# The rest of the second layer's modulation, moved from the first layer's down projections to the second layer's input projection

## The chip, the core and the metric

The kernel runs on one core of a Trainium2 chip. The metric is the device time of one launch in microseconds (us), and lower is better. The core has a matrix engine (PE, with its weight loads shown apart as PEld), VectorE (DVE), ScalarE (ACT), GpSimd (POOL), and SyncE (SP), whose queue issues nearly all DMA transfers of this program. All engines run side by side, each one through its own instructions in order, and they wait for one another by semaphores.

## The reference, cut to what matters

One step of a two-layer trunk over 1152 tokens (128 context tokens and 1024 latent ones) of width 1024. Each layer is

```python
sh1, sc1, gt1, sh2, sc2, gt2 = split(silu(c) @ w_ada + b_ada)      # modulation, for c and for c_ctx
y = rmsnorm(x, g1) * (1 + sc1) + sh1
x = x + gt1 * (mixers(y @ w_in) @ w_out)                            # attention, mLSTM, attention
y = rmsnorm(x, g2) * (1 + sc2) + sh2
a, g = split(y @ w_up)
x = x + gt2 * ((silu(conv(g)) * a) @ w_down)                        # gated FFN
```

The modulation of a layer depends on `c` and `c_ctx` and on its own weights alone, so it can be computed at any time before its first use. `sh1` and `sc1` are used when the layer begins, the other four after that layer's mixers.

## The kernel before, in words

Everything is kept transposed: 128 channels on the partitions, tokens along the free dimension, in three chunks of 384 tokens. Products are made to nearly full float32 precision by splitting each factor into a high part and a low part (`split`, L104: ACT casts the high part, L108; DVE or POOL subtracts it for the low part, L109) and by three matmuls per product. Weights come through `weight` (L111): one 512 KB transfer into a staging tile `stg` (2 buffers), ACT makes `wh`, POOL makes `wl` (4 buffers each).

The order of the work is that of the calls in the source. The framework's scheduler may interleave what is independent; an instruction wrapped in `pin` stays behind all that was traced before it on its engine. A DMA waits on SP's queue until the buffer that it fills is free, and everything behind it on that queue waits with it.

The stages that matter here, in order of time:

- **First layer's input projection** (`project_a` with l = 0). Nine slots of projection and mixer preparation; first-layer modulation is woven between them (`modulation`, L210): 64 steps, each a 256 KB transfer of transposed `w_ada` rows into `stm` and two DVE instructions of 128x512 (L221) that multiply by the broadcast silu(c) row `cb` and sum along the free dimension. `MODS` sets how many steps each slot takes.
- **First layer's up projections** (`Up.run`). 22 steps of matmuls; `Up.modulation` (L1426) gives the second layer's modulation as a list of 96 units of the same kind (48 groups of 128 outputs by two halves of the 1024 inputs; L1453, two pinned DVE instructions per unit), and `some_mod` takes 52 of them here.
- **First layer's down projections** (`down_units`, L1533). For each of the three token chunks, 22 steps of 24 matmuls (L1556) into all eight PSUM banks. Each step's `fetch` (L1538) loads a `w_down` tile and a 128x384 tile `hst` of the hidden activations and splits both; four buffers of each lie ahead of PE. After each step, `some_mod` takes what is left of the modulation, 44 units over 63 steps. In a step that takes a unit, the low part of `hst` (`hs`, L109) is made on POOL, in the others on DVE. At the end of a chunk DVE adds the eight PSUM banks to `x` (L1603); the next chunk's matmuls need the banks free. The norm for the second layer (L308 and L311 among others) is spread over the next chunk's steps.
- **Second layer's input projection** (`project_a` with l = 1), with no modulation in it.
- The second layer's mixers, out projection, up projections, and its **down projections**: the same code as in the first layer, with no modulation left to do and a lighter final norm (L1619).

The units' tiles (`stm`, three buffers; `cb`, one; `mjk`, one; the sums `mds`) lie in a pool `md`, which is released after the down projections. `half(h)` (L1440) loads one half of `cb` and applies Silu on ACT; the sums of the first input half go into the modulation tile itself, and `fin` adds both halves and the bias.

Of the kernel before, what the change touches and what calls it, by code (L numbers as in the profile page):

```python
# [50 lines left out]
def kernel(ctx: ExitStack, tc: tile.TileContext, A, O, layers=L):  # L51
# [458 lines left out]
        return [unit(i, c) for c in range(3) for i in range(2)], tiles  # L510


    def project_a(S, l, y, Z, first):
        vec = vecs[l]

        count, free = [0], []
# [199 lines left out]
        if l == 0:  # L716
            cb = conditioning(S)
            mod = [u for i in range(2, 6) for u in modulation(S, l, i, cb)]
        done = 0
        for i, slot in enumerate(slots):  # L720
            upto = sum(MODS[:i + 1]) * len(mod) // sum(MODS)
            weave(slot, mod[done:upto])
            done = upto

# [498 lines left out]
    class Up:  # L1223
# [196 lines left out]
                share -= unit  # L1420
                f()

        def mods_left(self):
            return sum(u for u, f in self.mod)

        def modulation(self, mp):  # L1426

            l = self.l + 1
            groups = [range(16), range(16, 48)]
            loads = [(h, m) for ms in groups for h in range(2) for m in ms]  # L1430
            wq, st = [], dict(s=(mods[l], mp.tile([128, 48, 2], F32, tag="mds", name="mds", bufs=1)))

            def load():
                if loads:
                    h, m = loads.pop(0)
                    w = mp.tile([128, 512], F32, tag="stm", name="stm", bufs=3)
                    sync.dma_start(out=w, in_=A["w_adat"][l, m, :, h * 512:(h + 1) * 512])
                    wq.append(w)

            def half(h):  # L1440
                def f():
                    st["cb"] = mp.tile([128, 2, 512], F32, tag="cb", name="cb", bufs=1)
                    sync.dma_start(out=st["cb"], in_=A["crow"][:, h * 512:(h + 1) * 512].unsqueeze(0).to_broadcast([128, 2, 512]))
                    act.activation(out=st["cb"], in_=st["cb"], func=AF.Silu)
                return 0, f

            def unit(h, m):
                def f():
                    load()
                    w = wq.pop(0)  # L1450
                    for j in range(2):
                        o = w if j else mp.tile([128, 512], F32, tag="mjk", name="mjk", bufs=1)
                        pin(dve.scalar_tensor_tensor(out=o, in0=w, scalar=1.0, in1=st["cb"][:, j], op0=ALU.mult, op1=ALU.mult,  # L1453
                                                     accum_out=st["s"][h][:, m, j:j + 1]))
                return 1, f

            def fin(ms):
                def f():
                    a, b = (t[:, ms.start:ms.stop] for t in st["s"])
                    bias = vecs[l][:, V_BADA + ms.start:V_BADA + ms.stop]  # L1460
                    dve.tensor_tensor(out=b, in0=a, in1=b, op=ALU.add)
                    dve.tensor_tensor(out=a, in0=b, in1=bias.unsqueeze(2).to_broadcast([128, len(ms), 2]), op=ALU.add)
                return 0, f
            load()
            load()
            return [u for ms in groups for u in [v for h in range(2) for v in [half(h)] + [unit(h, m) for m in ms]] + [fin(ms)]]

        def run(self):
            S, l = self.S, self.l
            oq, tn = self.ops[:2]  # L1470
            sq2, rstd2, scale2 = self.norm()
            S.rings = dict(sA=[0, 1], sB=[2, 3], sD=[4, 5], u1=[6, 7])
            self.bk = {}
            run(sq2)
            rstd2[0]()
            rstd2[1]()
            run(scale2)
            dbg(f"xm{l}", self.x)
            tn.release()
            oq.release()  # L1480
            fp = self.new_pool("f", "left")
            self.mp = None
            if l + 1 < layers:
                self.mp = self.new_pool("md", "left")
                self.mod = self.modulation(self.mp)
                self.some_mod(0)

            def tiles():
                self.tiles = {k: fp.tile([128, n], F32, tag=k, name=k, bufs=1) for k, n in (("gb", 1156), ("lb", T), ("tg", 1156))}
                conv_pad(self.tiles["gb"])  # L1490
            for n in range(NFF):
                tiles()
                nxt = n + 1 < NFF
                if n == 0:
                    for p in ("P1", "P6", "P2", "P5", "P7", "C22", "P3", "P4", "C21"):
                        self.step(n, p)
                    self.load(1)
                    self.step(n, "G2")
                    self.prep(1, "g")
                    self.step(n, "L2")  # L1500
                    self.prep(1, "s")
                    self.prep(1, "t1")
                else:
                    self.prep(n, "a")
                    self.step(n, "P1")
                    if nxt:
                        self.load(n + 1)
                    self.step(n, "G2")
                    self.step(n, "P2")
                    self.step(n, "P6")  # L1510
                    if nxt:
                        self.prep(n + 1, "g")
                    self.some_mod(2)
                    self.step(n, "P7")
                    self.step(n, "P5")
                    self.step(n, "C22")
                    if nxt:
                        self.prep(n + 1, "s")
                    self.some_mod(1 - n % 2)
                    self.step(n, "L2")  # L1520
                    self.step(n, "P3")
                    if nxt:
                        self.prep(n + 1, "t1")
                    self.step(n, "P4")
                    self.step(n, "C21")
                if n + 1 < NFF:
                    self.tail(n)
            self.p5.release()
            self.p4.release()
            self.p3.release()  # L1530
            return fp

    def down_units(S, l, x, Z, hp, up, scale):  # L1533
# [4 lines left out]
        def fetch(lo_eng=dve):  # L1538
            if len(ready) == len(steps):
                return  # L1540
            c, k = steps[len(ready)]
            wt = weight(A["w_down"][l, k])
            s = S.t.tile([128, CH], F32, tag="hst", name="hst", bufs=3)
            sync.dma_start(out=s, in_=Z.h[k, :, csl(c)])
            h = hp.tile([128, 2, CH], F32R, tag="hs", name="hs", bufs=4)
            split(s, h[:, 0], h[:, 1], act, lo_eng)
            ready.append((*wt, h))
# [31 lines left out]
            fetch()  # L1579
        up.tail(NFF - 1)  # L1580
        fetch()
        rs, left, nmod = {}, [], up.mods_left()
        for c in range(3):
            D = {}
            for k in range(NFF):
                for m in range(8):
                    mul(D, c * NFF + k, m)
                i, total = c * NFF + k, len(steps) - 3
                share = (i + 1) * nmod // total - i * nmod // total if i < total else 0
                if k < NFF - 1:  # L1590
                    fetch(pool if share else dve)
                up.some_mod(share)
                if left and k in (1, 2) or k > 3:
                    run(left[:1])
                    del left[:1]
            if c == 2:
                S.rings = dict(u1=list(range(8)))
            acc = {}
            squares, rstd = stat_units(S, x, c, rs, acc)
            for m in range(8):  # L1600
                for a, b, j in pieces(c):
                    xs = x[:, m, c * CH + a:c * CH + b]
                    dve.scalar_tensor_tensor(out=xs, in0=D[m][:, a:b], scalar=mods[l][:, 40 + m, j:j + 1], in1=xs, op0=ALU.mult, op1=ALU.add)  # L1603
                squares[m]()
                if m == 3:
                    fetch(pool)
            left = (rstd if c == 2 else stats(c, acc)) + scale(c, rs)
        assert not up.mod
        return left

    def final_units(x, c, rs):
# [31 lines left out]
    for l in range(layers + 1):  # L1643
# [51 lines left out]
            run(left)  # L1695
        S.t.release()
        if l > 0:
            if up.mp:
                up.mp.release()
            fp.release()  # L1700
            fe.release()
        xp.release()
        if l < layers:
            Z = scratch(l)
            gp = new_pool("g", mine)
            G.col = gp.tile([128, 2, 5, 36], F32, name="gcol")
            G.M = gp.tile([128, T], F32R, name="gM")
            S.t = new_pool("ta", mine)
            project_a(S, l, yn, Z, first)
            S.t.release()  # L1710
            S.r.release()
        if l == layers:
# [180 lines left out]
```

## Time and profile before

| | us |
|---|---|
| Median of 3 runs | 3314.67 (3311.49 to 3322.43) |
| The profiled execution's own time | 3314.44 |
| Its span, first to last instruction | 3312.6 |
| PE busy | 3137.3 (95%) |
| DVE busy | 2254.8 (68%) |
| POOL busy | 1463.8 (44%) |
| ACT busy | 1517.8 (46%) |

Matmuls are pipelined, so their busy spans overlap and a busy PE need not run at its best rate. A column PEclk gives the granted clock of PE in a stretch, as a share of 2.4 GHz. In the rows of groups, the number after the bar is the busy time, then the mean of one in ns, then the idle time of the engine just ahead of them with what ended it.

### The profile page before, as it was taken

The page shows a single profiled execution, that of the slowest core. Times are in us where ns is not written, and L with a number is a line of the kernel's source. Part 1 is how long each engine was busy: PE and PEld are TensorE (multiplying, and loading weights), DVE is VectorE, ACT ScalarE, POOL GpSimd, SP SyncE. Part 2 cuts the span into 40 slices and gives each one's busy share as a digit, 9 for nine tenths or more (in the row PEclk, how much of TensorE's full clock was granted, in tenths as well). Part 3 has the DMA queues.
Part 4 walks back from the last instruction along what each step waited for, and adds up shares of the span by engine and source line. Part 5 has one row for each costly group of instructions (what it writes and reads, how often), then busy time and mean ns, then how long its engine had stood idle before and what let it go on. Part 6 is the DMA issues. An engine that isn't in the chain of part 4 may idle for free.

```text
span 3312.6 us, 50639 instructions
## 1 busy us (share of the span) xinstructions
PE 3137.3 (95%) x18433; PEld 3007.9 (91%) x18433; DVE 2254.8 (68%) x4674; ACT 1517.8 (46%) x2994; POOL 1463.8 (44%) x1155
## 2 busy tenths in 40 slices
PE   7989999999899999989799999899998999999998
PEld 4879988999799999889799899789997999999998
DVE  5983788887777777667755137988886444446665
ACT  5433456775533333333335333677754333333432
POOL 4213233122466666577662122331323655565664
PEclk9999999999899999999899999999998999999999
DMA  6565334110133233555542353342201222124553
GB/s 245 167 201 178 101 95 134 50 51 22 56 107 109 96 112 99 156 186 180 183 158 87 112 168 104 91 127 52 58 13 55 71 74 77 63 80 157 183 173 129
DMA packets 210973, 377.40 MB, mean 114 GB/s; under 512 B 37618, under 2 KB 138146, under 8 KB 210338
## 3 DMA queue, kind: packets, MB, share of 16 engines
q1 hardware_dynamic: 210722, 374.16, 35.4%
q8 instruction: 145, 2.38, 0.3%
q14 instruction: 106, 0.87, 0.1%
HBM read 294.86 MB, written 79.51 MB: 113 GB/s over the span
## 4 chain that ended last, share of the span: by engine, by line
PE 72%; DVE 15%; ACT 4%; issue 4%; DMA 3%; POOL 3%; SPq 0%; DVEq 0%; POOLq 0%; ACTq 0%
PE u L122 23%; PE dn L1556 10%; PE sB L1365 8%; PE sD L1365 5%; PE sA L1365 5%; PE sc L122 4%; PE pv L988 4%; PE u L369 4%; PE tr L971 3%; DVE stm L1453 2%; POOL wl L109 1%; DVE mjk L1453 1%; DMA stg<-in_w_down 1%; DVE hs L109 1%; PE u L246 1%
## 5 line engine op out<-in xcount | busy, mean ns | idle before, releaser
L109 POOL TENSOR_TENSOR wl<-stg,wh 128x1024 fp32r<-128x1024 f32 (+1 forms) x364 | 841.5, 2313 | 676.3 <-ACT wh L108 648.2
L108 ACT CAST wh<-stg 128x1024 fp32r<-128x1024 f32 (+1 forms) x370 | 348.9, 943 | 607.1 <-DVE stg L1256 164.8
L1556 PE MATMUL dn<-hs,wh 128*128 128x384 f32 x2112 | 554.2, 343 | 39.7 <-DVE x L1603 15.7
L1556 PEld LDWEIGHTS dn<-hs,wh 128*128 128x128 f32 x2112 | 392.7, 194 | 45.8 <-POOL hs L109 12.0
L122 PE MATMUL u<-yh,wh 128*128 128x384 f32 x1088 | 369.5, 340 | 5.7 <-ACT yh L310 4.4
L122 PE MATMUL u<-yl,wh 128*128 128x384 f32 x1088 | 369.2, 339 | 1.1 <-POOL yl L109 0.6
L122 PE MATMUL u<-yh,wl 128*128 128x384 f32 x1088 | 367.8, 338 | 0.1
L1556 PE MATMUL dn<-hs,wl 128*128 128x384 f32 x1056 | 359.8, 341 | 0.0
L109 DVE TENSOR_TENSOR hs<-hst,hs 128x384 fp32r<-128x384 f32 x85 | 166.4, 1964 | 170.5 <-ACT hs L108 170.5
L948 DVE TENSOR_SCALAR_CACHE_REDUCE p<-sc,rq 128x384 f32<-128x384 f32 (+1 forms) x400 | 232.1, 597 | 17.4 <-PE sc L122 16.0
L975 DVE TENSOR_TENSOR pt<-tr,pt 128x384 fp32r<-128x384 f32 (+1 forms) x400 | 212.9, 539 | 10.8 <-ACT pt L974 7.5
L122 PEld LDWEIGHTS u<-yh,wh 128*128 128x128 f32 x1088 | 207.4, 191 | 9.5 <-ACT yh L310 6.5
L122 PEld LDWEIGHTS u<-yl,wh 128*128 128x128 f32 x1088 | 207.3, 191 | 4.9 <-DVE yl L311 3.1
L122 PEld LDWEIGHTS u<-yh,wl 128*128 128x128 f32 x1088 | 207.6, 191 | 0.4 <-issue 0.2
L974 ACT CAST pt<-tr 128x384 fp32r<-128x384 f32 (+1 forms) x400 | 175.2, 468 | 69.5 <-PE tr L971 67.5
L1556 PEld LDWEIGHTS dn<-hs,wl 128*128 128x128 f32 x1056 | 204.3, 194 | 0.0
L988 PE MATMUL pv<-pt,v 128*128 128x256 f32 (+1 forms) x1184 | 187.1, 293 | 5.4 <-DVE v L109 2.3
L971 PE MATMUL tr<-cst,p 128*128 128x128 f32 x1168 | 185.5, 276 | 4.7 <-DVE pt L975 4.7
L960 ACT ACTIVATE p<-p,mx 128x1152 f32<-128x1152 f32 (+1 forms) x144 | 167.6, 1164 | 47.2 <-DVE mx L958 43.8
L109 POOL TENSOR_TENSOR wl<-ws,wh 128x512 fp32r<-128x512 f32 x88 | 126.9, 1442 | 114.8 <-ACT wh L108 107.0
L988 PEld LDWEIGHTS pv<-pt,v 128*128 128x128 f32 x1184 | 162.4, 193 | 15.5 <-ACT pt L974 6.0
L971 PEld LDWEIGHTS tr<-cst,p 128*128 128x128 f32 x1168 | 142.7, 142 | 20.1 <-DVE pt L975 10.5
(378 smaller groups left out, 8132.5 us busy)
## 6 DMA issues: line engine op xcount, KB each, us to landing
stg<-in_w_down SPq DMA_DIRECT2D x132, 512.0 KB
stg<-in_w_up SPq DMA_DIRECT2D x88, 512.0 KB
stm<-in_w_adat SPq DMA_DIRECT2D x160, 256.0 KB
hst<-z_h SPq DMA_DIRECT2D x132, 192.0 KB
z_h<-tg SPq DMA_DIRECT2D x44, 512.0 KB
stg<-in_w_in SPq DMA_DIRECT2D x32, 512.0 KB
x<-in_x SPq DMA_DIRECT2D x6, 1536.0 KB
qk<-z_qk SPq DMA_DIRECT2D x24, 384.0 KB
```

Of the source, the lines that this page charges most:

```text
L108: act.copy(out=hi, in_=src)
L109: (lo_eng or dve).tensor_tensor(out=lo, in0=src, in1=f32(hi), op=ALU.subtract)
L122: pe.matmul(ps, lhsT=a, rhs=b, start=(i == 0), stop=(i == n - 1))
L369: pe.matmul(ps, lhsT=pairs[q][0], rhs=pairs[q][1], start=(q == 0), stop=(q == 3 * n - 1))
L948: dve.tensor_scalar(out=st["p"][:, b * m:(b + 1) * m], in0=ps, scalar1=G.rq[:, 0 if h < 4 else h - 3, j:j + 1], scalar2=None, op0=ALU.mult ...
L960: act.activation(out=p, in_=p, func=AF.Exp, scale=-1.0, bias=mx, accum_out=pair["s"][:, w[4]:w[4] + 1])
L971: pe.transpose(ps[:, t * 128:(t + 1) * 128], p[:, (3 * g + t) * 128:(3 * g + t + 1) * 128], ident)
L974: act.copy(out=hi, in_=p3)
L975: dve.tensor_tensor(out=lo, in0=p3, in1=f32(hi), op=ALU.subtract)
L988: pe.matmul(pair["ps"][:, :m], lhsT=pr[q][0], rhs=pr[q][1], start=(q == 0), stop=(q == 2 * n - 1))
L1365: pe.matmul(ps, lhsT=a, rhs=c, start=start and q == 0, stop=q == 11, skip_group_check=True)
L1556: pe.matmul(D[m][:, :CH], lhsT=a, rhs=b, start=k == 0 and q == 0, stop=k == NFF - 1 and q == 2, skip_group_check=True)
```

## The change

`Up.modulation` is given a plan. With `first=True` it lists the 52 units that run beside the up projections; with `first=False` the 44 others: 12 of the first input half and 32 of the second, with a `cb` load ahead of each half and one `fin` at the end, 47 entries. `project_a` for the second layer takes that second list, in its own pool, and spreads it evenly over its nine slots. `down_units` no longer runs modulation, and all its `fetch` calls inside the steps make the low part of `hst` on DVE. The pool `md` is released at the end of the up projections.

```diff
@@ project_a
-    def project_a(S, l, y, Z, first):
+    def project_a(S, l, y, Z, first, rest):
...
+        elif rest:
+            mod = [f for u, f in rest(S.t, False)]
         done = 0
         for i, slot in enumerate(slots):
-            upto = sum(MODS[:i + 1]) * len(mod) // sum(MODS)
+            upto = sum(MODS[:i + 1]) * len(mod) // sum(MODS) if l == 0 else (i + 1) * len(mod) // len(slots)
             weave(slot, mod[done:upto])
@@ Up
-        def modulation(self, mp):
+        def modulation(self, mp, first=True):
             l = self.l + 1
-            groups = [range(16), range(16, 48)]
-            loads = [(h, m) for ms in groups for h in range(2) for m in ms]
+            plan = [(0, range(16)), (1, range(16)), (0, range(16, 36))] if first else [(0, range(36, 48)), (1, range(16, 48))]
+            loads = [(h, m) for h, ms in plan for m in ms]
...
-            return [u for ms in groups for u in [v for h in range(2) for v in [half(h)] + [unit(h, m) for m in ms]] + [fin(ms)]]
+            return [u for h, ms in plan for u in [half(h)] + [unit(h, m) for m in ms] + [fin(ms)] * h]
@@ Up.run, at its end
+            assert not self.mod
+            if mp:
+                mp.release()
@@ down_units
-                i, total = c * NFF + k, len(steps) - 3
-                share = (i + 1) * nmod // total - i * nmod // total if i < total else 0
                 if k < NFF - 1:
-                    fetch(pool if share else dve)
-                up.some_mod(share)
+                    fetch()
@@ the main loop
-            project_a(S, l, yn, Z, first)
+            project_a(S, l, yn, Z, first, up.modulation if l else None)
```

## Rows read from the trace of the kernel before

**Rows 1.** The page, busy time of each engine over the whole span.

```profile
PE 3137.3 (95%) x18433; PEld 3007.9 (91%) x18433; DVE 2254.8 (68%) x4674; ACT 1517.8 (46%) x2994; POOL 1463.8 (44%) x1155
```

**Rows 2.** Busy time by stretch: down projections of the first layer, then the second.

```profile
core 0: us, PE busy (x) PEld busy (x) DVE busy (x) ACT busy (x) POOL busy (x), PEclk, DMA share, GB/s
1374.50:1707.60 333.10, 299.67 (x1608) 293.80 (x1609) 222.06 (x294) 116.26 (x181) 236.37 (x123) 0.93 0.55 182
3011.60:3294.70 283.10, 280.22 (x1609) 278.26 (x1607) 181.68 (x136) 106.70 (x159) 171.55 (x77) 0.99 0.52 170
```

**Rows 3.** Down-projection matmuls (L1556), first layer: what PE's idle time before them ended with.

```profile
  DVE x L1603: 22.6, 4
  POOL hs L109: 22.6, 10
  ACT hs L108: 19.2, 7
  DVE hs L109: 4.6, 3
```

**Rows 4.** The same for the second layer's down projections.

```profile
  DVE rsv L150: 3.6, 3
  issue: 1.4, 1
  DVE x L1603: 1.1, 1
```

**Rows 5.** Groups by shape, first layer's down projections (the stretch of rows 2).

```profile
L109 POOL TENSOR_TENSOR wl<-stg,wh 128x1024 fp32r<-128x1024 f32 x64 | 164.2, 2567 | 85.9 <-ACT wh L108 69.1 <-PE dn L1556 8.2 <-DMA hst<-z_h 4.4
L1453 DVE SCALAR_TENSOR_TENSOR stm<-stm,cb 128x512 f32<-128x512 f32 x44 | 77.7, 1765 | 1.2
L109 POOL TENSOR_TENSOR hs<-hst,hs 128x384 fp32r<-128x384 f32 x45 | 57.7, 1283 | 0.0
L1453 DVE SCALAR_TENSOR_TENSOR mjk<-stm,cb 128x512 f32<-128x512 f32 x44 | 54.3, 1233 | 5.8 <-ACT cb L1444 5.8
L109 DVE TENSOR_TENSOR hs<-hst,hs 128x384 fp32r<-128x384 f32 x21 | 31.8, 1521 | 84.4 <-ACT hs L108 84.4
```

**Rows 6.** Groups by shape, second layer's down projections.

```profile
L109 POOL TENSOR_TENSOR wl<-stg,wh 128x1024 fp32r<-128x1024 f32 x64 | 157.1, 2457 | 104.3 <-ACT wh L108 93.4 <-PE dn L1556 10.7
L109 DVE TENSOR_TENSOR hs<-hst,hs 128x384 fp32r<-128x384 f32 x60 | 130.7, 2182 | 80.8 <-ACT hs L108 80.8
L1619 DVE SCALAR_TENSOR_TENSOR x<-x,gfin,rsb 128x384 f32<-128x384 f32 x12 | 16.0, 1383 | 4.3 <-ACT rsb L1574 4.3
```

**Rows 7.** DVE's busy time in the first layer's down projections by L308, then L311.

```profile
1374.50:1707.60 333.10, 12.54 (x18) 0.93 0.55 182
...
1374.50:1707.60 333.10, 13.22 (x18) 0.93 0.55 182
```

**Rows 8.** First layer's down projections, their start: PE in order, then SP's queue.

```profile
1374.47 2.22 PE L1556 MATMUL dn<-hs,wh 128*128 128x384 f32 x5 [7.82 <-ACT hs L108]
...
1360.68 7.65 SPq L113 DMA_DIRECT2D stg<-in_w_down  x2
1368.39 1.37 SPq L1544 DMA_DIRECT2D hst<-z_h  x3
```

**Rows 9.** Busy time by stretch: like parts of the two input projections (columns of rows 2).

```profile
93.90:268.60 174.70, 158.88 (x820) 145.76 (x820) 139.39 (x360) 64.36 (x116) 39.19 (x23) 0.93 0.58 187
1755.70:1912.00 156.30, 153.26 (x820) 143.08 (x820) 55.29 (x106) 64.48 (x116) 35.73 (x23) 0.97 0.31 104
```

**Rows 10.** First layer's input projection: modulation by shape, then PE's longest wait.

```profile
L221 DVE SCALAR_TENSOR_TENSOR stm<-stm,cb 128x512 f32<-128x512 f32 x61 | 46.2, 757 | 0.9
L221 DVE SCALAR_TENSOR_TENSOR mjk<-stm,cb 128x512 f32<-128x512 f32 x61 | 45.1, 739 | 3.9 <-DMA stm<-in_w_adat 3.8
...
168.81 0.69 PE L122 MATMUL u<-cn1h,wh 128*128 128x384 f32 x1 [6.69 <-DVE gcol L485]
```

**Rows 11.** A new half of `cb` in the down projections: ACT, then DVE.

```profile
1463.62 1.06 ACT L1444 ACTIVATE cb<-cb 128x1024 f32<-128x1024 f32 x1 [7.81 <-DMA cb<-in_crow]
...
1464.71 0.70 DVE L1453 SCALAR_TENSOR_TENSOR mjk<-stm,cb 128x512 f32<-128x512 f32 x1 [5.76 <-ACT cb L1444]
```

**Rows 12.** Table loads on ACT in the second layer's input projection, the last two.

```profile
1752.08 1.28 ACT L413 ACT_TABLE_LOAD   x1
1753.38 0.31 ACT L413 ACTIVATE g_e<-g_e 36x128 f32<-36x128 f32 x1
1761.72 1.28 ACT L681 ACT_TABLE_LOAD   x1
```

More of the change, by code (lines that the diff above doesn't have):

```diff
@@ L1421, in some_mod @@
                 f()
-        def mods_left(self):
-            return sum(u for u, f in self.mod)
-        def modulation(self, mp):
+        def modulation(self, mp, first=True):
             l = self.l + 1
-            groups = [range(16), range(16, 48)]
-            loads = [(h, m) for ms in groups for h in range(2) for m in ms]
+            plan = [(0, range(16)), (1, range(16)), (0, range(16, 36))] if first else [(0, range(36, 48)), (1, range(16, 48))]
+            loads = [(h, m) for h, ms in plan for m in ms]
             wq, st = [], dict(s=(mods[l], mp.tile([128, 48, 2], F32, tag="mds", name="mds", bufs=1)))
@@ L1481, in run @@
             fp = self.new_pool("f", "left")
-            self.mp = None
+            mp = None
             if l + 1 < layers:
-                self.mp = self.new_pool("md", "left")
-                self.mod = self.modulation(self.mp)
+                mp = self.new_pool("md", "left")
+                self.mod = self.modulation(mp)
                 self.some_mod(0)
@@ L1581, in down_units @@
         fetch()
-        rs, left, nmod = {}, [], up.mods_left()
+        rs, left = {}, []
         for c in range(3):
@@ L1607, in down_units @@
             left = (rstd if c == 2 else stats(c, acc)) + scale(c, rs)
-        assert not up.mod
         return left
@@ L1697 @@
         if l > 0:
-            if up.mp:
-                up.mp.release()
             fp.release()
```

## The prediction

> **What bounds the kernel now.** I began with busy time. PE works in 95% of the span [rows 1], so what counts is where it still waits or runs at the lower clock. The program has its own control experiment: both layers run the same down projections, with modulation beside them in the first layer only. By stretch, the first layer takes 333.1 us and the second 283.1 for the same work, 1608 and 1609 matmul records, and the granted clock is 0.93 against 0.99 of 2.4 GHz [rows 2]. In the second layer PE is busy for 280.2 of the 283.1 us: there PE itself is the bound. In the first it is not, and the waits say why: PE sat idle 22.6 us until DVE had emptied the PSUM banks into x, 22.6 until POOL and 19.2 until ACT had delivered the split activations [rows 3]. In the second layer the same list holds a few us [rows 4].
>
> The groups by shape show the crowding. The 44 units are 88 DVE instructions with means of 1.77 and 1.23 us [rows 5]; the same operation takes 0.76 and 0.74 us in the first layer's input projection [rows 10], where POOL is busy 39 of 175 us [rows 9] and not 236 of 333 [rows 2]. So DVE and POOL hold each other up in the down projections: DVE spends 77.7 + 54.3 = 132 us on modulation there that would need 88 x 0.75 = 66 us elsewhere. On top, 45 low parts went to POOL (57.7 us) to spare DVE, and POOL is then late with both kinds of low part.
>
> **The change, step by step.** The sum is made against the profiled execution, 3314.4 us of its own time; the median of the runs, 3314.7, is the same.
>
> Taken out of the first layer's down projections: 88 DVE instructions (132 us of DVE), 44 transfers of 256 KB and one `cb` load with its Silu on SP and ACT. The 45 low parts go from POOL back to DVE. Both engines then have the load of the second layer: POOL 171.6 of 283, DVE 181.7 of 283 [rows 2], where DVE's 60 low parts, at a mean of 2.18 us because they wait for POOL, hide under PE [rows 6]. One thing differs: the first layer also norms for the next layer, 12.5 + 13.2 = 25.8 us of DVE [rows 7] against 16.0 for the final norm [rows 6]. DVE would be at about 192 of 283 us, still far from PE. The body falls by 333.1 - 283.1 = 50.0 us if that extra is covered. Bounds for what stays: 0, and 10 us if all the extra DVE time came out on PE. I take 4, nearer to the covered end, since DVE has some 90 us free.
>
> The start: PE waits 7.8 us before the first down matmul, until ACT has cast activations whose loads SP issued at 1368.4, behind two weight loads that held its queue for 7.65 us [rows 8]. The second layer shows no wait on ACT's cast at that place [rows 4]. In the first layer the pool `md` pushes the tiles of `hst` to other addresses; with `md` released they take its place and wait only for the last units. Between 0 and 7.8 us gained; I take 5, since the order on SP's queue can stay bad.
>
> The up projections keep their 52 units in the same order: 0, hidden as now under PE's matmuls.
>
> Added to the second layer's input projection: 44 units, thus 88 DVE instructions at the 0.75 us of rows 10 = 66 us, on a DVE that is busy 55.3 of 156.3 us in the like part [rows 9], with 44 transfers, two `cb` loads (one more than is taken away) and two Silus. In number this fits: 55 + 66 = 121 of 156. But DVE serves the mLSTM gates and the convolutions just there, and PE waits for them. The trace has this case too: the first layer runs the same 820 matmuls with 122 such instructions in 174.7 us, and the second in 156.3 without any [rows 9, 10]. The difference is 18.4 us, its largest piece a wait of 6.7 us for a PSUM copy that stood behind modulation on DVE [rows 10], with the clock at 0.93 against 0.97. Bounds: 0, where free DVE time takes it all, and 18.4. Scaled by count, 88/122 x 18.4 = 13.3. The placing speaks for the upper half as well: by `MODS` the first layer puts 37 of its 68 steps into the first seven slots, where gates and convolutions are, and the even spread will put 36 of 47 entries there. I take 13.
>
> New waits: the units are pinned, so what stands behind one on DVE waits when its `stm` load or `cb` is late. The second half of `cb` comes in slot 2. In the down projections such a change held ACT for 7.8 us (its queue was waiting for the load) and DVE for 5.8 [rows 11]. Here gates, convolution and PSUM copies stand behind; PE has the 72 matmuls of a projection tile between producer and user, 72/820 x 156.3 = 13.7 us [rows 9]. Bounds: 0 to 5.8 us; I take 0, with cover in the matmuls of the next slot. SP issues 46 more transfers, at under half a us each (1.37 us for three [rows 8]), behind waits of its own; the DMA share was 0.31 [rows 9], against 0.58 in the first layer.
>
> The second Silu falls between Tanh calls on ACT, so that its table must be loaded and the other one loaded again. The rows show 1.28 us for a load, with the next instruction right behind it [rows 12]: two loads, 2.6 us on an ACT that is busy 64 of 156 us [rows 9], off PE's path; 0 taken, 2.6 the upper end.
>
> The Trainium skill ("ScalarE: Activation LUTs", "What ACT_TABLE_LOAD costs") counts 2.66 us for every switch, a drain of some 1.38 us included; by that it would be an estimated 5.3 us of ACT and the upper end 2.7 us higher. The rows here do not show the drain.
>
> Sum: -50 + 4 - 5 + 13 = -38 us; 3314.4 - 38 = **3276 us**. Best ends: -50 - 7.8 + 0 = -58, 3257. Worst: -50 + 10 + 18.4 + 5.8 + 2.6 = -13, 3301.
>
> **The rivals.** *Hidden outright:* the even spread, one slot earlier, and the pin keep modulation out of the way of the gates and the projection pays 0 to 3 us. For it: DVE has 100 us free there [rows 9]. Against it: the first layer's 18.4. Time: -50 + 4 - 5 + 2 = -49, 3265.
>
> *The down projections give back only part:* modulation was one load among several, and the next-layer norm (POOL and ACT work in it too) keeps bunching at the chunk ends, so that the waits for x [rows 3] stay, 22.6 us of the 50. For it: the second layer has no such norm. Against it: DVE was behind with modulation in those waits. Time: -38 + 19 = -19, 3295.
>
> *Slower:* a convoy on pinned units. A unit whose load sits behind a wait on SP stops DVE; gates and PSUM copies behind it come late, SP's next entries wait for those, and PE drains. In the down projections a unit cost DVE 1.77 + 1.23 = 3.0 us [rows 5]; if it did so here, DVE would need 55 + 44 x 3.0 = 187 us, 31 beyond the 156, and the total would still be -51 + 31 = -20. The other side begins where DVE needs 156 + 51 = 207 us, at (207 - 55) / 44 = 3.5 us a unit. At 4.5 us, DVE needs 253: +97 - 51 = +46, 3360. Against it: in the first layer DVE waited for these loads 3.8 us in all [rows 10], with four buffers where there are now three.
>
> **How the numbers follow.** The forecast 0.66, hidden outright 0.16, part only 0.12, the convoy 0.04, and 0.02 for a small part of the gain or none, as where modulation drifts past the projection into the mixers and delays them. A measurement of this kernel tells about 0.3%, 10 us, from no change. Faster beyond that: the first two whole and nearly all of the third, 0.92; same 0.03; slower 0.05. The range goes from the best end, 3257, to the worst, 3301, and holds the first three cases.
>
> **What would show it.** Right: the first layer's down projections at 284 to 292 us with a clock near 0.99, few waits for x and hs, DVE near 190 us; the first cast of hst before the last up matmul; the second layer's like part at 165 to 175 us with its DVE near 125, and its modulation instructions at means under 0.8 us. Wrong: down projections still over 300 us; or the like part beyond 185 us, with DVE idle until `stm` or `cb` arrives. The forecast falls if the projection gives back over 30 us, or if a later stage of the second layer grows.

## The result, and the profile after

The changed kernel takes 3280.2 us (median of 4 runs, 3273.4 to 3282.2), the kernel before 3317.2 (4 runs): a ratio of 0.9888, with a 95% interval from 0.9867 to 0.9908. The forecast was 3276, with a range from 3257 to 3301. The profiled execution spans 3280.5 us, against 3312.6.

The table cuts the span at landmarks on PE: the first up-projection matmul of the first layer, the first and last down matmul, the first gate transpose of the second layer's input projection (L421), and the first matmul of the next stage (L369). Between the last two lies the like part of [rows 9].

| us | before | after | difference |
|---|---|---|---|
| up to the first layer's up projections | 835.7 | 839.4 | +3.7 |
| up projections, up to the first down matmul | 538.8 | 532.7 | -6.1 |
| down projections, first to last matmul ("the body") | 333.0 | 289.1 | -43.9 |
| from there to the first gate transpose | 48.2 | 44.9 | -3.3 |
| like part of the input projection ("the part") | 156.4 | 177.8 | +21.4 |
| all that follows | 1400.5 | 1396.5 | -4.0 |
| sum | 3312.6 | 3280.5 | -32.1 |

The first and the last row hold no changed code. Over all profiles of this study the first lies between 833.4 and 839.4, and the last between 1393.0 and 1400.5, but for one version below whose units delay what follows (1404.8). So differences of this size say nothing.

Busy time of the changed kernel by stretch, the body and then the part; the lines answer to [rows 2] and [rows 9].

```profile
core 0: us, PE busy (x) PEld busy (x) DVE busy (x) ACT busy (x) POOL busy (x), PEclk, DMA share, GB/s
1372.10:1661.60 289.50, 283.50 (x1610) 281.48 (x1611) 194.47 (x163) 119.69 (x185) 179.15 (x83) 0.98 0.55 176
1706.10:1883.90 177.80, 159.13 (x819) 146.53 (x820) 121.16 (x272) 71.16 (x124) 36.76 (x23) 0.92 0.47 152
```

The body is now PE's own: 283.5 us busy of 289.5, the clock at 0.98 where it was 0.93. PE's idle time has fallen from 33.4 to 6.0 us, and its busy time for the same matmuls by 16 us, with the higher clock. DVE's 194 us and POOL's 179 have room. In the part, DVE's busy time has gone from 55 to 121 us, and the clock has fallen from 0.97 to 0.92.

PE's matmuls of the first layer's down projections, before and after, with what ended PE's own idle time ahead of them:

```profile
L1556 PE MATMUL dn<-hs,wh 128*128 128x384 f32 x1056 | 284.4, 350 | 37.1 <-DVE x L1603 14.7 <-POOL hs L109 10.6 <-ACT hs L108 9.0
L1558 PE MATMUL dn<-hs,wh 128*128 128x384 f32 x1056 | 271.9, 338 | 5.0 <-DVE hs L109 2.4 <-ACT hs L108 1.5 <-DVE x L1602 1.1
```

PE waited 37.1 us before and 5.0 after; for x it was 14.7 and is 1.1. The wait of 7.8 us ahead of the first matmul is part of the 9.0 on ACT, and in the table it lies in the row of the up projections. The larger figures of [rows 3] and [rows 4] add the idle time of the weight loads (PEld) to that of the matmuls, so that most waits stand in them twice. The prediction read them as PE's alone.

The units beside the input projection, by shape, in the part (they answer to the units of [rows 5], and to those of the first layer in [rows 10]):

```profile
L1452 DVE SCALAR_TENSOR_TENSOR stm<-stm,cb 128x512 f32<-128x512 f32 x41 | 34.7, 846 | 0.9
L1452 DVE SCALAR_TENSOR_TENSOR mjk<-stm,cb 128x512 f32<-128x512 f32 x40 | 31.2, 779 | 5.7 <-DMA stm<-in_w_adat 5.3 <-ACT cb L1443 0.3
```

Beside the down projections their means were 1.77 and 1.23 us. Here, with POOL busy 37 of 178 us, they are 0.85 and 0.78. The trace shows what the difference is. Beside the down projections, 24 of the 88 instructions had no POOL instruction running at the same time; they took 0.68 us on average and 0.70 at most, and the 64 others took 1.80. Beside the input projection, 74 of 88 ran without POOL and took 0.69 us, the 14 others 1.58.

PE's longest waits in the part, in order of time:

```profile
1709.09 0.25 PE L421 MATMUL u<-cst,g_f 36*128 36x36 f32 x1 [2.70 <-DVE g_f L419]
...
1759.60 0.44 PE L122 MATMUL u<-yh,wh 128*128 128x384 f32 x1 [3.99 <-ACT kv L388]
...
1783.81 0.69 PE L122 MATMUL u<-cn1h,wh 128*128 128x384 f32 x1 [3.31 <-DVE gcol L485]
...
1819.98 0.58 PE L122 MATMUL u<-wh,cn1h 128*128 128x256 f32 x1 [7.39 <-ACT kv L665]
```

They add up to 17.4 us. Before the change the part had one wait of over half a us, of 3.0 us at the place of the fourth:

```profile
1849.22 0.39 PE L122 MATMUL u<-wh,cn1h 128*128 128x256 f32 x1 [3.04 <-ACT kv L665]
```

By each of these waits lies a stretch in which the granted clock is 0.5 (1.2 GHz): 3.4, 3.4, 10.2 and 10.2 us long, 27 us in all, against 10 in the part before the change. In them one 128x384 matmul follows the other after 0.32 us, elsewhere after 0.18. The third stretch begins 3 us before its wait does, and before the change 6.8 us of the lower clock lie at the same place without any wait.

The first wait comes from SP's queue. The loads of the gates (L406) stood there behind three `stm` loads, 8.2 us behind the store that they read from; before the change it was 2.5 us.

```profile
1691.11 7.70 SPq L1436 DMA_DIRECT2D stm<-in_w_adat  x3
...
1698.90 0.36 SPq L406 DMA_DIRECT2D g_a<-z_gates  x1
```

The third is of the forecast's kind: the gates' PSUM copy stood behind units on DVE. The second is of two kinds. ACT's queue ahead of it:

```profile
1754.22 1.17 ACT L681 ACTIVATE ta<-gb 128x1153 f32<-128x1153 f32 x1 [9.48 <-DVE gb L393]
1755.41 1.28 ACT L1443 ACT_TABLE_LOAD   x1
1757.07 1.06 ACT L1443 ACTIVATE cb<-cb 128x1024 f32<-128x1024 f32 x1 [0.38 <-DMA cb<-in_crow]
1758.04 1.13 ACT L108 CAST cn1h<-kv 128x1152 fp32r<-128x1152 f32 x1
1759.08 0.47 ACT L388 COPY kv<-u 128x384 f32<-128x384 f32 x1
```

ACT's evacuation of a PSUM bank (L388), for which PE waits, stood in ACT's queue behind a Tanh of the convolution (L681). This one waited for DVE, where four units stood ahead of the convolution. Behind the Tanh came the table load and the Silu of the second half of `cb`, 2.6 us together, of which only 0.4 are a wait for its load, and then a cast. The chain ahead of the fourth:

```profile
1814.02 0.71 DVE stm L1452 x2
1814.74 0.33 SPq L1436
...
1816.64 2.82 DMA z_kn<-kv
1819.56 0.38 ACT kv L665
```

A `stm` load waited on SP for a unit to free its buffer. The stores of `kn` stood behind it on the same queue, the buffers that they empty stayed full, ACT could not empty PSUM into them, and PE stopped.

### The profile page after: what moved, and what is told of

Read it like the earlier page. It is cut to its first block, busy times and chain, and to the rows that moved or that the text cites. A ratio compares the mean times of both kernels' runs of the same rounds, so it can differ in the third digit from the quotient of the medians.

```text
span 3280.5 us, 50657 instructions
## 1 busy us (share of the span) xinstructions
PE 3124.5 (95%) x18433; PEld 2994.4 (91%) x18433; DVE 2292.0 (70%) x4717; ACT 1522.1 (46%) x2997; POOL 1401.7 (43%) x1112
## 4 chain that ended last, share of the span: by engine, by line
PE 75%; DVE 14%; DMA 3%; ACT 3%; issue 3%; POOL 2%; SPq 0%; DVEq 0%; POOLq 0%; ACTq 0%
PE u L122 21%; PE dn L1558 15%; PE sB L1367 8%; PE sD L1367 5%; PE sA L1367 5%; PE sc L122 5%; PE u L369 4%; PE pv L990 4%; PE tr L973 4%; DVE mjk L1452 1%; DMA stm<-in_w_ada 1%; DVE stm L1452 1%; DVE ssq L271 1%; PE m L1149 1%; PE m L1138 1%
## 5 line engine op out<-in xcount | busy, mean ns | idle before, releaser
L109 POOL TENSOR_TENSOR wl<-stg,wh 128x1024 fp32r<-128x1024 f32 (+1 forms) x364 | 832.7, 2289 | 697.6 <-ACT wh L108 685.9
L1558 PE MATMUL dn<-hs,wh 128*128 128x384 f32 x2112 | 541.8, 337 | 7.6 <-DVE hs L109 2.4
L1558 PEld LDWEIGHTS dn<-hs,wh 128*128 128x128 f32 x2112 | 383.5, 189 | 10.4 <-issue 2.7
L109 DVE TENSOR_TENSOR hs<-hst,hs 128x384 fp32r<-128x384 f32 x128 | 267.5, 2095 | 158.5 <-ACT hs L108 158.3
```

Of the source, the lines that this page charges most:

```text
L109: (lo_eng or dve).tensor_tensor(out=lo, in0=src, in1=f32(hi), op=ALU.subtract)
L1558: pe.matmul(D[m][:, :CH], lhsT=a, rhs=b, start=k == 0 and q == 0, stop=k == NFF - 1 and q == 2, skip_group_check=True)
```

## The experiments

Two questions: what made the body 44 us shorter, and what makes the part 21 us longer. The body first. All bodies and parts are between the landmarks of the table.

**Short units before.** The units' DVE work cut to 16 of 512 columns, in the kernel before; everything else stays.

```diff
-                        pin(dve.scalar_tensor_tensor(out=o, in0=w, scalar=1.0, in1=st["cb"][:, j], op0=ALU.mult, op1=ALU.mult,
+                        n = 16 if m >= 36 or (h and m >= 16) else 512
+                        pin(dve.scalar_tensor_tensor(out=o[:, 0:n], in0=w[:, 0:n], scalar=1.0, in1=st["cb"][:, j, 0:n], op0=ALU.mult, op1=ALU.mult,
```

> The kernel before with the 44 units beside the down projections cut to 16 of their 512 columns on DVE (the output is not the reference's); transfers, buffers, pinned places and the routing of low parts to POOL stay. Theory DVE time: the units' 132 us of DVE are what makes the body 333 us; then it falls to 290 to 302 us. Rival, the queue: 44 transfers of 256 KB that wait for their buffers hold SP's queue, so that w_down comes late; then the body stays over 315 us.

The body fell to 301.0 us, the launch to 3273.3 (one run).

```profile
1374.50:1675.50 301.00, 288.08 (x1607) 285.45 (x1608) 130.80 (x295) 118.16 (x185) 218.76 (x124) 0.96 0.62 204
```

PE's down matmuls in it, with the ends of its own idle time:

```profile
L1557 PE MATMUL dn<-hs,wh 128*128 128x384 f32 x1056 | 275.7, 342 | 16.8 <-DVE x L1604 8.4 <-ACT hs L108 7.8 <-POOL hs L109 0.6
```

So 32 of the 43.9 us hang on the units' DVE time, with the routing to POOL in place. PE's waits for POOL's hs are nearly gone and those for x down to 8.4 us; the 7.8 us are the wait ahead of the first matmul, outside the body. What of the other 12 us (301.0 against 289.1) is due to transfers, to `cb` or to the routing was not told apart. This kernel also keeps the pool; against the version below that keeps it without units (284.1), 17 us are left.

**DVE alone for hs, before.** The other half of the change undone: units stay, the low parts all go to DVE.

```diff
-                    fetch(pool if share else dve)
+                    fetch()
```

> The kernel before with all low parts of hst on DVE and the 44 units still beside the first layer's down projections: the other half of the change undone. If DVE and POOL are one crowded pair, moving 44 low parts from POOL to DVE changes little: body 325 to 340 us. Rival, POOL's lateness (22.6 us of PE's waits) was the cause: 305 to 320 us. Rival the other way, DVE in order behind pinned units delays every low part: over 345 us.

> The kernel before with all low parts of hst on DVE and the units still beside the down projections, timed; one look gave 3286 us with a body of 310.0 us. If the routing to POOL is worth what that look showed, the ratio to the kernel before is 0.988 to 0.994, half to nearly all of the change's own gain. Rival, that look was a chance: 0.997 to 1.003.

The body was 310.0 us in the first profile and 314.8 in the second, which is the rival's range: POOL's lateness. Timed, the kernel takes 3293.9 us, a ratio to before of 0.9928, 0.9906 to 0.9950. One argument of one call, with no unit moved, gives 0.72% where the change gives 1.12%, about two thirds.

```profile
1371.00:1681.00 310.00, 289.25 (x1607) 285.24 (x1608) 251.83 (x330) 116.77 (x180) 176.84 (x80) 0.96 0.61 195
```

The same rows here:

```profile
L1556 PE MATMUL dn<-hs,wh 128*128 128x384 f32 x1056 | 277.0, 343 | 26.0 <-DVE x L1603 14.2 <-ACT hs L108 7.8 <-DVE rsv L150 2.0
```

DVE is busier than ever, 252 of 310 us, and PE waits less all the same: POOL has fallen from 236 to 177 us, and PE's 10.6 us of waits for its `hs` are gone. The waits for x stay, 14.2 us here and 15.5 in the second profile. No wait of PE ended with `wl`, before the change or here.

**POOL for hs, after.** The routing alone put back into the changed kernel.

```diff
+                i, total = c * NFF + k, len(steps) - 3
+                share = l == 0 and i < total and (i + 1) * 44 // total - i * 44 // total
                 if k < NFF - 1:
-                    fetch()
+                    fetch(pool if share else dve)
```

> The changed kernel with the low parts of hst made on POOL again in the 44 of 63 steps where they were before the change (first layer only). The down projections' body, first to last matmul, took 333.0 us before and 289.1 after the change. If POOL was a bound of its own there, 44 more instructions of some 1.0 us bring it from 179 to about 223 us of busy time, wl comes late and the body takes 294 to 305 us. Rival, that only DVE was short and the routing to POOL was a symptom: 286 to 291 us.

```profile
1366.40:1656.00 289.60, 282.37 (x1607) 279.95 (x1608) 108.11 (x120) 119.88 (x186) 222.63 (x126) 0.99 0.54 176
```

289.5 us, and 289.1 without it: the rival. The body of the changed kernel, in eight profiles that share its code up to there, lies between 287.9 and 289.3, so POOL with 223 us and no units on DVE costs nothing that can be told, and DVE drops to 108 us. The routing is bad only together with the units, where it costs 18 to 23 us.

**The pool kept.** `md` released after the down projections, as before the change.

```diff
-            if mp:
-                mp.release()
...
+            if up.mp:
+                up.mp.release()
             fp.release()
```

> The changed kernel with the pool of the units kept until the first layer's down projections have ended, as before the change; nothing else differs. If the wait of 7.8 us ahead of the first down matmul came from where the tiles of hst lie, it comes back (6 to 9 us, where the changed kernel has 1.9 and 2.7) and the launch is 4 to 7 us longer. Rival, that the wait came from modulation's transfers on SP's queue: it stays under 4 us.

The wait is back, and yet nothing is lost. The first down matmul of this kernel, then of the changed one:

```profile
1371.06 2.22 PE L1556 MATMUL dn<-hs,wh 128*128 128x384 f32 x5 [7.83 <-ACT hs L108]
```

```profile
1372.11 1.32 PE L1558 MATMUL dn<-hs,wh 128*128 128x384 f32 x6 [1.53 <-ACT hs L108]
```

With the pool kept, up projections and body take 537.6 + 284.1 = 821.7 us; with the early release 532.7 + 289.1 = 821.8, and between 818.3 and 823.1 in the eight profiles with that code. The launch took 3275.8 us (one run), inside the changed kernel's own runs, where 4 to 7 us more had been expected. Released early, PE begins 6 us sooner and then waits 2.4 us for the next low part on DVE; its busy time in the body is 2 us longer as well, at a clock of 0.98 against 0.99.

**No units.** The 44 units left out of the input projection.

```diff
-            mod = [f for u, f in rest(S.t, False)]
+            dve.tensor_copy(out=mods[l][:, 16:48, :], in_=vec[:, V_BADA + 16:V_BADA + 48].unsqueeze(2).to_broadcast([128, 32, 2]))
```

> The changed kernel with the 44 units left out of the second layer's input projection (the modulation columns that they would fill get the bias alone, so the output is not the reference's). The part of that projection from the first gate transpose to the first matmul of the next stage took 156.4 us before the change and 177.7 after it. If the units are the whole price there, it returns to 156 to 158 us and the launch to about 3259 (3280 - 21). Rival, that part of the 21 us comes from somewhere else, as from tiles placed otherwise or from what the down projections leave behind: the part stays over 163 us.

```profile
1702.20:1863.00 160.80, 155.00 (x821) 144.56 (x821) 57.44 (x106) 64.57 (x117) 35.49 (x23) 0.96 0.30 102
```

The part is 160.8 us, between the two expectations: the units cost 17.0 of the 21.4, and 4.4 remain without them. They lie ahead of the last gate transposes (L481): from the first ones to there PE took 61.8 us, against 57.5 before. With no unit and no `cb` PE waits 2.6 us for the same evacuation as in the second wait above, and 3.4 us at the lower clock begin there:

```profile
1749.84 0.69 PE L122 MATMUL u<-yh,wh 128*128 128x384 f32 x1 [2.64 <-ACT kv L388]
```

Why ACT is late there without units stays open; the part took 154.6, 154.6 and 156.2 us in the three variants of the kernel before. The launch took 3263.8 us (one run).

**Short units after.** The same cut as above, in the changed kernel's input projection; only the condition differs.

```diff
+                        n = 512 if first else 16
...
```

> The changed kernel with each of the 44 units cut to 16 of its 512 columns on DVE; every transfer, buffer and pinned place stays (the output is not the reference's). Theory DVE time: the 21 us come from 88 instructions of 0.69 us that stand ahead of gates, convolutions and PSUM copies; then the part falls to 157 to 163 us. Rival, the queue: they come from the 44 transfers of 256 KB and the wait for a new half of cb, which hold SP's queue and the pinned instructions behind them; then the part stays at 168 to 178 us.

```profile
1700.10:1863.90 163.80, 153.58 (x820) 142.70 (x820) 71.09 (x264) 68.10 (x119) 35.79 (x23) 0.97 0.50 168
```

163.9 us, just over the end that I had given to DVE time: 13.9 of the 17.0 us are DVE's time, and transfers, pins and `cb` without it cost 3.1 (one profile each; parts with like code differ by up to 2 us). The wait ahead of `kn`, too, falls from 7.4 to 2.9 us, about what it was before the change, although all 44 loads are still issued: buffers come free at once when units are short. The queue is how the delay travels, and DVE's time is what feeds it.

**No pins.** The 44 units not pinned, placing as in the change.

```diff
-                        pin(dve.scalar_tensor_tensor(out=o, in0=w, scalar=1.0, in1=st["cb"][:, j], op0=ALU.mult, op1=ALU.mult,
+                        (pin if first else (lambda x: x))(dve.scalar_tensor_tensor(out=o, in0=w, scalar=1.0, in1=st["cb"][:, j], op0=ALU.mult, op1=ALU.mult,
```

> The changed kernel with the 44 units not pinned, so that the scheduler may put other DVE instructions ahead of them or them ahead of others, as in the first layer's projection; placing is even as in the change. If the wait for cb and for stm behind pinned instructions is a large part of the 21 us, the part from the first gate transpose to the next stage falls from 177.7 to 165 to 171 us. Rival, DVE's own time decides, as the short units showed (163.8 us with all pins in place): 174 to 184 us.

> The changed kernel with the 44 units not pinned, timed; one look gave 3264.8 us, with the part at 172.3 us where the pinned one has 177.7 and 44 us more even starts of the units. If leaving the pin out is worth what that look showed, the median is 3263 to 3272 us and the ratio to the kernel before 0.984 to 0.987, below the changed kernel's 0.9888. Rival, the look was a fast one among runs that spread by 9 us, and DVE's time alone decides: 3273 to 3282 us, 0.987 to 0.990.

The part took 172.2 us in the first profile, between the two ranges expected, and 174.2 in the second. Counted from the first gate transpose, the units begin at about the same place (14 us ahead of it, with pins 13) and end 40 us earlier, after 125 and 127 us and not 167. Timed it is 3271.2 us, 0.9857 (0.9833 to 0.9881). That is below the changed kernel's 0.9888 and in the range expected if the pin costs, but the intervals overlap, and 3.6 to 5.6 us of the part is all that the profiles show. I count the pin as a small cost, not proven. ("44 us" in the second expectation is a slip for the 44 units.)

**Other places for the units.** Three versions that keep them away from the gates: the last three slots as 1 : 2 : 2, then as 2 : 2 : 1, then by hand.

```diff
-            upto = sum(MODS[:i + 1]) * len(mod) // sum(MODS) if l == 0 else (i + 1) * len(mod) // len(slots)
+            wt = MODS if l == 0 else [0, 0, 0, 0, 0, 0, 1, 2, 2]
+            upto = sum(wt[:i + 1]) * len(mod) // sum(wt)
```

```diff
-            upto = sum(MODS[:i + 1]) * len(mod) // sum(MODS) if l == 0 else (i + 1) * len(mod) // len(slots)
-            weave(slot, mod[done:upto])
+            upto = sum(MODS[:i + 1]) * len(mod) // sum(MODS) if l == 0 else sum([4, 5, 4, 0, 0, 0, 0, 20, 14][:i + 1])
+            cut = len(slot) - 2 * (l > 0 and i == 8)
+            weave(slot[:cut], mod[done:upto])
+            run(slot[cut:])
```

> The changed kernel with the 47 entries woven only into the last three of the nine slots (1 : 2 : 2), behind the gates and convolutions. If the price lies in what stands behind modulation in the first six slots, the part falls to 157 to 166 us and the launch to 3261 to 3272. Rival: the units don't fit beside the last slots (47 entries of 1.5 us are 70 us of DVE, the last three slots last some 87), run over into the mixers and give the gain back there: 3278 to 3290.

> The changed kernel with the 47 entries in the last three slots as 2 : 2 : 1, so that fewer of them stand ahead of uq_rope, whose DVE instructions made PE wait 5.4 us with 1 : 2 : 2 (3270 us measured, profile 3263). If that wait goes, the launch takes 3260 to 3268 us. Rival: more units beside ukv_k and ukv_v hold the stores of kn on SP's queue, and PE waits there instead: 3268 to 3276.

> The changed kernel with the 47 entries placed by hand: 13 (the first input half) in slots 0 to 2, none in slots 3 to 6, 20 in slot 7 and 14 beside the rest of the v projection in slot 8, ahead of uq_nope and uq_rope. Nothing then stands beside ukv's stores (waits of 4.0 and 7.5 us in the two late versions) or ahead of uq's weight and rotation (5.8 and 6.8 us). If these waits go and the early 13 cost 3 us, the launch takes 3260 to 3266 us. Rival, the early 13 delay the gates as the even spread did (some 6 us) and slot 7 runs over: 3267 to 3276.

| | launch, us | ratio to before | part, us | all that follows, us |
|---|---|---|---|---|
| the change (even) | 3280.2 | 0.9888 (0.9867 to 0.9908) | 177.8 | 1396.5 |
| 1 : 2 : 2 | 3270.5 | 0.9863 (0.9847 to 0.9880) | 159.5 | 1404.8 |
| 2 : 2 : 1 | 3268.2 | 0.9856 (0.9839 to 0.9872) | 170.6 | 1397.7 |
| by hand | 3267.2 | 0.9854 (0.9838 to 0.9870) | 169.1 | 1394.1 |

With 1 : 2 : 2 the part is nearly that of no units, and the mixers pay some 8 us, since uq_rope's rotation on DVE stands behind the last units:

```profile
1868.27 0.69 PE L369 MATMUL u<-yh,wh 128*128 128x384 f32 x1 [5.42 <-DVE ta L189]
```

With 2 : 2 : 1 that wait is gone. PE waits instead where the rival said, for the stores of kn, and also for uq's low part on DVE; the time lies at the lower end of the rival's range:

```profile
1798.26 0.58 PE L122 MATMUL u<-wh,cn1h 128*128 128x256 f32 x1 [7.18 <-ACT kv L665]
...
1858.85 0.69 PE L122 MATMUL u<-cn0h,wl 128*128 128x384 f32 x1 [6.45 <-DVE wl L109]
```

By hand, the waits at these two places are 2.8 and 3.5 us, but the 13 early entries cost the gates 5 to 9 us against the 3 expected, as the rival had it: from the first gate transposes to the last ones PE took 66.5 us, with even placing 67.7, with 1 : 2 : 2, which has no unit there, 57.5, and with no units at all 61.8. All three versions took 10 to 13 us less than the change, 8 to 11 by the ratios. Each one's interval still overlaps a little with that of the change; they agree among themselves. Their medians of 3267 to 3271 us, with that of the units not pinned, are the best seen that compute everything, and the 3260 to 3264 us of no or short units (one run each) is what hiding them outright would give.

## Why the prediction was right, point by point

- **The down projections.** The second layer as a control was the right reading: the body came to 289.1 us against 283.0 there. Forecast -50 + 4, measured -43.9. The waits named were the right ones, but PE's own were 14.7 us for x, 10.6 for POOL and 9.0 for ACT, not the 22.6, 22.6 and 19.2 that [rows 3] gives with the weight loads. The sum does not use these; the rival "part only" does.
- **The start.** Forecast -5 at that place, measured -6.1, and keeping the pool brings the 7.8 us back, though no run shows that the addresses of the tiles are the reason. The sign set for this place was missed: the first cast of hst, at 1371.6 us, still lies behind the last up matmul, at 1370.3. And as a term of the sum it was wrong, since the gain is not kept: the body is 5.0 us longer for it. Both terms together were forecast as -51 and came to -50.0 (871.8 to 821.8 us), because the body without that displaced wait, 284.1, is shorter than I had it.
- **The input projection.** Forecast 13 from bounds of 0 and 18.4, with the first layer as the second control; the part grew by 21.4 us, over the upper bound, 17.0 of it by the units and 4.4 without them. The 13 was meant for everything that the units do there; that their DVE time alone came to 13.9 (short units) is near it partly by chance. The step that failed is the terms set to 0 beside it. "PE has the 72 matmuls of a projection tile between producer and user" did not cover the change of `cb`, since what waited was ACT's emptying of PSUM, not a producer of data: 2.6 us of ACT's queue ahead of a wait of 4.0. And the loads and stores behind `stm` on SP's queue were in no term: waits of 2.7 us and of 7.4 - 3.0 = 4.4 us, and stretches at the lower clock beside them. The sign set for this place, 165 to 175 us, was missed; that for being wrong, over 185, was not met.
- **The tables.** Two more loads on ACT, 15 in the launch and not 13, the second of them ahead of an Exp of the gates and not of a Tanh, each of 1.28 us. The first is not off PE's path, as the prediction had it: it stands in ACT's queue ahead of the wait of 4.0 us.
- **The sum.** Forecast -38; the profile shows -32.1, the medians -37.0. The profiled execution was the longest among runs from 3273.4 to 3282.2. That the medians come within 1 us of the forecast is partly luck: the input projection cost 8.4 us more than its term.
- **The rivals.** "Hidden outright" fell: the units cost 17.0 us and not 0 to 3, and even the versions placed best pay some 3 to 11 us over no units or short ones. "Part only" fell: PE's waits for x went from 14.7 to 1.1 us. The convoy showed itself, at the gates' loads and in the `kn` stores, with 2.7 and 4.4 us where some 51 more on PE would have been needed to turn the sign.

What the forecast did not see is that the gain has two keys. The units make DVE late; the routing to POOL, there to spare DVE, made POOL late as well, and its undoing alone gives 0.9928. I had put both down as one relief.

## What to carry to other kernels

Where the same stage runs twice with a side job in only one of them, the pair prices the job's place: here the old place to within 2 us, the new one 8 us too low. Before moving a side job, try its companions on their own: a workaround that routes work to a second engine can cost more than the job that it was meant to help, and undoing it may be a one-word change. A moved job's price at the new place is its engine time and also the queues that it enters: look for what stands behind its loads and its table functions, above all stores and PSUM evacuations.

## What the runs showed that was not expected

- POOL with 223 of 290 us busy beside PE costs nothing that can be told when DVE has 108, and some 20 us when DVE has the units as well: the share of neither engine alone says so. DVE's low parts with a mean of 2.08 us in the changed kernel's body are harmless.
- A wait of 7.8 us on PE's path was removed at one place without a gain that can be told: 821.8 against 821.7 us over the two stages.
- The lower clock adds to the waits: by waits of 2.7 to 7.4 us PE ran at 1.2 GHz for 3.4 to 10.2 us. Not all of that is the waits' doing, since 6.8 us of it stood at one of these places before the change, with no wait there.
- Beside the down projections the units' DVE instructions took 1.80 us on average with a POOL instruction running at the same time and 0.68 without, and the profile counts the difference as busy time of DVE.
